# Reordering the six products of two channel tiles in a split-precision projection

## The chip, the cores and the metric

The kernel runs on one core of one Trainium2 chip. The metric is the device time of one execution in microseconds (us); times are compared by their medians over several runs.

## The reference

A decoder trunk of two residual layers over a sequence of 1024 tokens with 1024 channels, all in float32, and a final RMSNorm:

```
def reference(x, ...):
    for i in range(DEPTH):                       # DEPTH = 2
        h = rms_norm(x, norm_g[i])
        if i % N_MIXERS == 0:
            x = x + lru_mixer(h, ...)
        else:
            x = x + fox_mixer(h, ...)
    return rms_norm(x, final_g)

def lru_mixer(h, ...):                           # 1536 channels = 12 blocks of 128
    u = h @ w_in
    xb, gate = u[..., :1536], u[..., 1536:]
    xc = causal_depthwise_conv(xb, conv_w, conv_b)
    r = sigmoid(block_diag_linear(xc, wa, ba)); i = sigmoid(block_diag_linear(xc, wx, bx))
    a = exp(-8 * r * softplus(-a_param))
    hs = associative_scan(a, sqrt(1 - a**2) * (i * xc))
    return (hs * silu(gate)) @ w_out

def fox_mixer(h, ...):                           # 16 heads of 64
    q, k, v, gate, f_logit = split(h @ w_in)
    logits = q @ k.T / 8 + forgetting term from cumsum(log_sigmoid(f_logit)), causal
    return (softmax(logits) @ v * silu(gate)) @ w_out
```

## The kernel before

Activations are held with channels on the 128 partitions and tokens along the free dimension, in two halves of 512 tokens. A projection takes 8 channel tiles of 128 (12 for the output of the first layer, 8 for that of the second) into one accumulator of 128x512.

Each factor of such a product is split into a high part and a low part, and three of the four partial products are summed: high weights by high input, low weights by high input, high weights by low input. In layer 1 (the LRU layer) and in the output projections the parts are float32 values rounded for TensorE (`fp32r`, the rows show f32); in the query, key and gate projections of layer 2 they are float16. The weights are the first factor of `matmul(o, w, x)`: they are loaded into the array (an LDWEIGHTS, engine PEld in the profile), and the input's 512 columns are streamed past them.

`gemm_steps` writes these products, and yields after every second channel tile, so that callers can lay other work between. Its callers, by the name of what they accumulate:

- `product`: `ups` and `gps`, the branch and the gate path of the LRU layer, 12 channel blocks `n`, weights `wh`/`wl`, inputs `hh`/`hl`. `ups` is used by the convolution, `gps` by the SiLU.
- `gates`: `gate`, the two block-diagonal gates of a channel block, weights `wgh`/`wgl`, inputs `xch`/`xcl`. Here the list has one pair only, and the same matrices are used for both halves of the tokens.
- `project_out`: `ops`, the first layer's output, two channel blocks at a time, inputs `yh`/`yl` (the last two blocks are written by `mm3`, elsewhere).
- `play`: `gps1` (printed as `gps` with inputs `h` and weights `w`, f16), the query, key and gate projections that fill the attention of layer 2.
- `partial`: `ops1` (printed as `ops` with `yhh`/`yhl`), most of the second layer's output, near the end.

A weight block is loaded by SyncE's queue, cast to the high part by ScalarE (`to_hi`, L57), and the low part is the difference, made by GpSimd or VectorE (`to_lo`, L110). The low parts `hl`, `xcl`, `yl` of the inputs are made by VectorE after the high parts by ScalarE. Buffers rotate: 3 for the raw weights `wf`, 4 each for `wh` and `wl`.

The order on each engine in layer 1 is set by the framework's list scheduler from the program's order and its own timing model. In layer 2 the attention is interleaved by hand: strings such as `ORDER` say at which places a step of the scores (`maxima`: S, then p, pp and the transposing DMA into pT), of the weighted sum (`weigh`: O) or a step of the filling projections comes, and each step is held behind the last matmul written before it. The values projection (`values`: vps) has its own order of products.

Of the kernel before, what the change touches and what calls it, by code (L numbers as in the profile page):

```python
# [40 lines left out]
def trunk(ctx: ExitStack, tc: tile.TileContext, xt, w0, wg, wo0, pc, gn, gf, w1, wv, wf, bf, wo1, out):  # L41
# [26 lines left out]
    def matmul(*args, **kw):  # L68
        pe[0] = nc.tensor.matmul(*args, **kw)  # L69
        return pe[0]  # L70
# [66 lines left out]
    def gemm_steps(ps, pairs, chunks=(slice(0, HALF),)):  # L137

        pairs = list(pairs)
        for cs in chunks:  # L140
            o = ps[:, cs]
            for i, ((wh, wl), (xh, xl)) in enumerate(pairs):
                matmul(o, wh, xh[:, cs], start=i == 0, stop=False)
                matmul(o, wl, xh[:, cs], start=False, stop=False)
                matmul(o, wh, xl[:, cs], start=False, stop=i == len(pairs) - 1)
                if i % 2:
                    yield

    def drain(gen):
# [7 lines left out]
    def gemm(*args):  # L157
        drain(gemm_steps(*args))
# [40 lines left out]
    with nullcontext(ExitStack()) as l0:  # L199
# [184 lines left out]
        def out_weights(g, d0):  # L384

            wt = loaded([4, P])
            for j in range(2):
                nc.sync.dma_start(wt[:, 2 * j : 2 * j + 2], wo0[d0 + j, :, 2 * g : 2 * g + 2])
            hi = wpool.tile([P, 4, P], F32R, tag="wh", name="wh")
            lo = wpool.tile([P, 4, P], F32R, tag="wl", name="wl")  # L390
            to_hi(hi, wt, nc.scalar)
            to_lo(lo, wt, hi, nc.vector)
            return [[(hi[:, 2 * j + i], lo[:, 2 * j + i]) for i in range(2)] for j in range(2)]
# [184 lines left out]
        wl = [w for d0 in range(0, KT, 2) for w in out_weights(NB // 2 - 1, d0)]  # L578
        for h, cs in enumerate(halves):
# [4 lines left out]
            for d0 in range(0, KT, 4):  # L584
                pts = []
                for db in range(d0, d0 + 4):
                    if db % 2 == 0:
                        two = ps.tile([P, 2, HALF], F32, tag="S", name="ops")
# [31 lines left out]
    with ExitStack() as l1:  # L620
# [56 lines left out]
        def play(units):  # L677

            for u in units:
                u["start"]()  # L680
                w, h = u["w"], u["h"]
                after_ = [v["w"] for v in plan[plan.index(u) + 1 :] if v["w"] is not w][:1]
                pt = ps.tile([P, HALF], F32, tag="g", name="gps1")
                for i, _ in enumerate(gemm_steps(pt, zip(w.cast(), hT[h]))):
                    for v in after_ if seen[0] is not None else ():
                        if h == u["first"] and i == u["load"]:
                            v.load()
                        if h == u["last"] and i in u["cast"]:
                            with tc.issue_after(seen[0].ins):
                                v.cast(u["cast"].index(i) + 1)  # L690
                    yield
                nc.vector.scalar_tensor_tensor(pt, pt, unit_w[:, 4 + w.b : 5 + w.b], rs1[h], ALU.mult, ALU.mult)
                u["use"](h, pt)
# [406 lines left out]
        def partial(todo):  # L1100

            for db, c in todo:
                split_out(db)
                if c if db < 2 else not c:
                    split_out(db + 1)

                kept = c == 0 and db > 3
                x = home(db) if kept else rpool.tile([P, HALF], F32, tag="R", name="xp")
                nc.gpsimd.dma_start(x, x1d[c, :, db])
                pt = ps.tile([P, HALF], F32, tag="g", name="ops1")  # L1110
                yield from gemm_steps(pt, zip(wo[db], [y1[c][pair] for pair in range(6)]))
                nc.vector.tensor_tensor(x, x, pt, ALU.add)  # L1112
                if not kept:
                    nc.gpsimd.dma_start(x1d[c, :, db], x)
# [265 lines left out]
```

## Time and profile before

| | |
|---|---|
| median of 3 runs | 1066.17 us |
| the 3 runs | 1066.57, 1062.53, 1066.17 us |
| the profiled execution's own time | 1067.16 us |
| its span | 1065.4 us |
| TensorE matmuls | 1028.7 us busy (97%), 5094 records |
| TensorE weight loads | 721.8 us (68%), 5094 records |
| VectorE, ScalarE, GpSimd | 784.2, 659.9, 92.2 us |
| mean granted TensorE clock | 0.993 |

The span is the time from the first to the last instruction in the profile; 1.8 us of the execution's own time lie outside it. Matmuls are pipelined: the duration of one (0.39 us for 512 columns) is longer than the distance between two starts, so a stream is read by the distance of the starts. A fast matmul stream is one with no idle time in front of its members. The first layer ends at about 450 us, the attention runs from about 500 us, the last output quarter ends the span.

### The profile page before, as it was taken

How to read it: one execution, taken by the hardware profiler on the slowest of the kernel's cores; microseconds unless marked ns; L12 is line 12 of the kernel's file. 1: busy time of each engine (PE TensorE's matmuls, PEld its weight loads, DVE VectorE, ACT ScalarE, POOL GpSimd, SP SyncE). 2: the span in 40 equal slices, each digit the busy share in tenths (PEclk: the TensorE clock that was granted, in tenths of full speed). 3: DMA queues.
4: the chain of work that ended last, by engine and by line, in shares of the span. 5: the costliest groups of instructions: out<-in, count | busy, mean ns of one | idle time of the engine just before them, and what ended most of it. 6: DMA issues, size and time to landing. Idle time of an engine off the chain costs nothing. (4 is left out here: it accounts for less than half of the span.)

```text
span 1065.4 us, 15063 instructions
## 1 busy us (share of the span) xinstructions
PE 1028.7 (97%) x5094; PEld 721.8 (68%) x5094; DVE 784.2 (74%) x1456; ACT 659.9 (62%) x1211; POOL 92.2 (9%) x87
## 2 busy tenths in 40 slices
PE   9999999999999999998999989999999989999997
PEld 6787878888888888765445556554755448577776
DVE  7789667667856868885878866888487874986575
ACT  8479666565656575567657655675466664764455
POOL 1311111012103110001000000000000000012100
PEclk9999999999999999999999999999999999999999
DMA  7112434233423311543688993998658984789984
GB/s 244 60 49 63 117 88 128 78 114 112 134 65 121 112 58 40 170 130 87 150 163 171 180 198 80 192 179 176 163 106 180 180 190 120 151 194 240 250 199 159
DMA packets 219805, 148.92 MB, mean 140 GB/s; under 512 B 161936, under 2 KB 174864, under 8 KB 219728
## 3 DMA queue, kind: packets, MB, share of 16 engines
q1 hardware_dynamic: 217328, 140.09, 54.2%
q0 software_dynamic: 2400, 7.87, 2.4%
q8 instruction: 40, 0.66, 0.3%
q14 instruction: 37, 0.30, 0.1%
HBM read 73.33 MB, written 11.67 MB: 80 GB/s over the span
## 5 line engine op out<-in xcount | busy, mean ns | idle before, releaser
L69 PE MATMUL gps<-h,w 128*128 128x512 f16 x1152 | 269.1, 380 | 1.3 <-DVE qkl L795 1.1
L69 PEld LDWEIGHTS <-w 128*128 128x128 f16 x1152 | 104.2, 98 | 126.4 <-issue 13.8
L57 ACT ACTIVATE p<-S,m 128x128 f32<-128x128 f32 (+7 forms) x128 | 94.5, 739 | 68.1 <-DVE m L965 30.6
L57 ACT ACTIVATE pp<-p,sums 128x128 f16<-128x128 f32 (+7 forms) x128 | 96.0, 769 | 34.7 <-DVE sums L977 18.5
L979 DVE SCALAR_TENSOR_TENSOR pp<-p,sums,pp 128x128 f16<-128x128 f32 (+7 forms) x128 | 102.5, 813 | 14.1 <-ACT pp L57 11.7
L69 PE MATMUL S<-T,U 96*128 96x512 f32 (+7 forms) x384 | 106.2, 385 | 5.0 <-ACT p L57 4.7
L69 PE MATMUL vps<-w,h 128*128 128x256 f16 (+1 forms) x768 | 92.3, 282 | 12.7 <-ACT w L57 8.3
L965 DVE CUSTOM_DVE_ANT_0 S<-S,mask 128x128 f32<-128x128 f32 (+7 forms) x128 | 96.9, 758 | 6.1 <-PE S L69 5.3
L110 POOL TENSOR_TENSOR wl<-wf,wh 128x512 fp32r<-128x512 f32 x46 | 70.9, 1545 | 324.3 <-ACT wh L57 254.3
L69 PEld LDWEIGHTS <-h 128*128 128x128 f16 x768 | 76.7, 101 | 28.0 <-issue 10.8
L69 PEld LDWEIGHTS S<-T,U 128*128 128x128 f32 (+1 forms) x384 | 67.7, 190 | 28.8 <-ACT p L57 13.6
L57 ACT CAST wh<-wf 128x512 fp32r<-128x512 f32 x88 | 51.7, 593 | 53.6 <-PE ops L69 27.1
L69 PE MATMUL ops<-yh,wh 128*128 128x512 f32 x192 | 76.8, 400 | 0.9 <-ACT yh L57 0.5
L69 PE MATMUL ups<-hh,wl 128*128 128x512 f32 x192 | 75.8, 395 | 1.8 <-POOL wl L110 1.8
L69 PE MATMUL ups<-hh,wh 128*128 128x512 f32 x192 | 76.4, 399 | 0.7 <-ACT hh L57 0.6
L69 PE MATMUL O<-pT,v 128*128 128x512 f16 (+3 forms) x396 | 71.0, 322 | 6.0 <-DMA pT<-pp 6.0
L69 PE MATMUL gps<-hh,wh 128*128 128x512 f32 x192 | 75.7, 394 | 0.8 <-ACT wh L57 0.8
L69 PE MATMUL ups<-hl,wh 128*128 128x512 f32 x192 | 76.1, 396 | 0.1
L69 PE MATMUL ops<-yh,wl 128*128 128x512 f32 x192 | 75.7, 394 | 0.1
L69 PE MATMUL gps<-hh,wl 128*128 128x512 f32 x192 | 75.5, 393 | 0.0
L69 PE MATMUL gps<-hl,wh 128*128 128x512 f32 x192 | 75.5, 393 | 0.0
L69 PE MATMUL ops<-yl,wh 128*128 128x512 f32 x192 | 74.6, 394 | 0.0
(196 smaller groups left out, 1883.5 us busy)
## 6 DMA issues: line engine op xcount, KB each, us to landing
wf<-in_w SPq DMA_DIRECT2D x106, 256.0 KB
wsf<-in_w SPq DMA_DIRECT2D x48, 256.0 KB
wf<-in_wo SPq DMA_DIRECT2D x64, 128.0 KB
T<-qkh SPq DMA_DIRECT2D x64, 128.0 KB
U<-qkh SPq DMA_DIRECT2D x64, 128.0 KB
x<-in_xt SPq DMA_DIRECT2D x16, 256.0 KB
wsf<-in_wv SPq DMA_DIRECT2D x16, 256.0 KB
x1d<-x SPq DMA_DIRECT2D x16, 256.0 KB
```

Of the source, the lines that this page charges most:

```text
L57: act[0] = op(*args, **kw)
L69: pe[0] = nc.tensor.matmul(*args, **kw)
L110: return eng.tensor_tensor(lo, src, f32(hi), ALU.subtract)
L965: nc.vector.tensor_tensor_reduce(S[:, :n], S[:, :n], mask[:, SEQ - n :], -1.0, -NEG, ALU.add, ALU.min, accum_out=m)
L979: nc.vector.scalar_tensor_tensor(both[:, :, 1], p, r, both[:, :, 0], ALU.mult, ALU.subtract)
```

## The change

In `gemm_steps` the channel tiles are taken two at a time. Before, each tile's three products stood together, in the order high by high, low weights by high, high weights by low input. Now, of two tiles, first come the two products of each tile with the weights' high part (by the input's high part, then by its low part), four in all; then the two with the weights' low parts. With a single pair (in `gates`) the order becomes high by high, high by low input, low by high. The number of products, their operands, the accumulators and the places of the yields stay.

```
-            for i, ((wh, wl), (xh, xl)) in enumerate(pairs):
-                matmul(o, wh, xh[:, cs], start=i == 0, stop=False)
-                matmul(o, wl, xh[:, cs], start=False, stop=False)
-                matmul(o, wh, xl[:, cs], start=False, stop=i == len(pairs) - 1)
-                if i % 2:
+            for i in range(0, len(pairs), 2):
+                two = pairs[i : i + 2]
+                for j, ((wh, wl), (xh, xl)) in enumerate(two):
+                    matmul(o, wh, xh[:, cs], start=i + j == 0, stop=False)
+                    matmul(o, wh, xl[:, cs], start=False, stop=False)
+                for j, ((wh, wl), (xh, xl)) in enumerate(two):
+                    matmul(o, wl, xh[:, cs], start=False, stop=i + j == len(pairs) - 1)
+                if len(two) == 2:
                     yield
```

What stands on the engines follows from this and from the scheduler. Three places on TensorE are shown; the numbers behind the names tell the buffers apart (`hh_171`/`hl_172` are the two parts of channel tile 0, `hh_173`/`hl_174` of tile 1; `wh_130`/`wl_131` are the weights of `ups`, `wh_139`/`wl_140` those of `gps`).

First, the start of the program behind the warm-up, where `ups` and `gps` of channel block 0 are interleaved. Before:

```order
L69 MATMUL ups_239<-hh_171,wh_130 128x512
L69 MATMUL ups_239<-hh_171,wl_131 128x512
L69 MATMUL ups_239<-hl_172,wh_130 128x512
L69 MATMUL ups_239<-hh_173,wh_130 128x512
L69 MATMUL ups_239<-hh_173,wl_131 128x512
L69 MATMUL ups_239<-hl_174,wh_130 128x512
L69 MATMUL gps_264<-hh_171,wh_139 128x512
L69 MATMUL ups_239<-hh_175,wh_130 128x512
L69 MATMUL ups_239<-hh_175,wl_131 128x512
L69 MATMUL gps_264<-hh_171,wl_140 128x512
```

And with the change, at the same place:

```order
L69 MATMUL ups_239<-hh_171,wh_130 128x512
L69 MATMUL ups_239<-hl_172,wh_130 128x512
L69 MATMUL ups_239<-hh_173,wh_130 128x512
L69 MATMUL ups_239<-hl_174,wh_130 128x512
L69 MATMUL ups_239<-hh_171,wl_131 128x512
L69 MATMUL ups_239<-hh_173,wl_131 128x512
L69 MATMUL gps_264<-hh_171,wh_139 128x512
L69 MATMUL gps_264<-hl_172,wh_139 128x512
L69 MATMUL gps_264<-hh_173,wh_139 128x512
L69 MATMUL gps_264<-hl_174,wh_139 128x512
L69 MATMUL ups_239<-hh_175,wh_130 128x512
L69 MATMUL gps_264<-hh_171,wl_140 128x512
```

The low input part `hl_172` is now second, where it was third; the low weights come fifth and sixth. Of `gps`, four products stand ahead of the next tile `hh_175` of `ups`, where one did.

Second, TensorE at the start of `ups` of channel block 5 (weights `wh_1290`/`wl_1291`; `ops` are products of the first layer's output). Before:

```order
L69 MATMUL ups_1300<-hh_171,wh_1290 128x512
L69 MATMUL ups_1300<-hh_171,wl_1291 128x512
L69 MATMUL ups_1300<-hl_172,wh_1290 128x512
L69 MATMUL ups_1300<-hh_173,wh_1290 128x512
L69 MATMUL ups_1300<-hh_173,wl_1291 128x512
```

With the change:

```order
L69 MATMUL ups_1300<-hh_171,wh_1290 128x512
L69 MATMUL ups_1300<-hl_172,wh_1290 128x512
L69 MATMUL ups_1300<-hh_173,wh_1290 128x512
L69 MATMUL ups_1300<-hl_174,wh_1290 128x512
L69 MATMUL ops_1130<-yh_591,wh_1118 128x512
L69 MATMUL ops_1130<-yl_592,wh_1118 128x512
L69 MATMUL ops_1130<-yh_771,wh_1118 128x512
L69 MATMUL ops_1130<-yl_772,wh_1118 128x512
L69 MATMUL ops_1130<-yh_591,wl_1119 128x512
L69 MATMUL ops_1130<-yh_771,wl_1119 128x512
L69 MATMUL ups_1300<-hh_171,wl_1291 128x512
L69 MATMUL ups_1300<-hh_173,wl_1291 128x512
```

Before, the product with the low weights `wl_1291` was the second of the block. Now four products with `wh_1290` and six of `ops` stand ahead of it.

Third, a projection in layer 2 (float16: `h16` and `w16` each hold both parts of a tile, so that the parts are not told apart by name). Here the weight loads are instructions of their own. Before:

```order
L69 LDWEIGHTS w16_4244
L69 MATMUL gps1_4239<-h16_3640,w16_4244 128x512
L69 LDWEIGHTS w16_4244
L69 MATMUL gps1_4239<-h16_3640,w16_4244 128x512
L69 LDWEIGHTS w16_4244
L69 MATMUL gps1_4239<-h16_3640,w16_4244 128x512
L69 LDWEIGHTS w16_4244
L69 MATMUL gps1_4239<-h16_3641,w16_4244 128x512
L69 LDWEIGHTS w16_4244
L69 MATMUL gps1_4239<-h16_3641,w16_4244 128x512
```

With the change:

```order
L69 LDWEIGHTS w16_4244
L69 MATMUL gps1_4239<-h16_3640,w16_4244 128x512
L69 LDWEIGHTS w16_4244
L69 MATMUL gps1_4239<-h16_3640,w16_4244 128x512
L69 LDWEIGHTS w16_4244
L69 MATMUL gps1_4239<-h16_3641,w16_4244 128x512
L69 LDWEIGHTS w16_4244
L69 MATMUL gps1_4239<-h16_3641,w16_4244 128x512
L69 LDWEIGHTS w16_4244
L69 MATMUL gps1_4239<-h16_3640,w16_4244 128x512
L69 LDWEIGHTS w16_4244
L69 MATMUL gps1_4239<-h16_3641,w16_4244 128x512
```

The products are in the new order, and each still has its own load. Counted over the whole program, both versions have the same instructions on every engine. Outside TensorE, 71 of 1435 rows of VectorE, 55 of 968 of ScalarE, 24 of 724 of SyncE and 2 of 92 of GpSimd stand elsewhere. Nearly all of these are in layer 1, in heads 13 to 15 and behind them; in the attention between these no row of VectorE, ScalarE, SyncE or GpSimd moves, and TensorE's units (each accumulator's group of products) follow one another as before.

## The prediction

> **What bounds the kernel now.** I read the page's head first, then busy time by stages, then the rows of the stages.
>
> ```profile
> span 1065.4 us, 15063 instructions
> PE 1028.7 (97%) x5094; PEld 721.8 (68%) x5094; DVE 784.2 (74%) x1456; ACT 659.9 (62%) x1211; POOL 92.2 (9%) x87
> ```
>
> TensorE (PE) is busy for 97% of the span, no other engine for more than 74%. Weight loads (PEld) are as many as matmuls. By stages (columns: length, then busy us and count of PE, PEld, DVE, ACT, POOL, then the granted clock, the DMA share, GB/s):
>
> ```profile
> 0.00:50.00 50.00, 47.50 (x192) 36.66 (x193) 35.21 (x42) 33.57 (x53) 11.59 (x14) 1.00 0.48 160
> 50.00:100.00 50.00, 49.86 (x216) 40.09 (x214) 46.22 (x60) 37.88 (x46) 6.27 (x4) 1.00 0.17 47
> 100.00:200.00 100.00, 97.43 (x416) 77.64 (x417) 63.19 (x69) 64.80 (x131) 18.13 (x12) 1.00 0.35 104
> 200.00:300.00 100.00, 100.00 (x435) 81.28 (x434) 73.43 (x75) 60.27 (x100) 16.54 (x11) 1.00 0.35 111
> 300.00:400.00 100.00, 100.00 (x434) 81.38 (x433) 67.34 (x68) 64.33 (x100) 19.11 (x12) 1.00 0.29 92
> ...
> 800.00:900.00 100.00, 93.16 (x524) 55.63 (x523) 72.14 (x173) 59.02 (x114) 0.00 (x0) 0.97 0.82 177
> 900.00:1000.00 100.00, 100.00 (x483) 69.65 (x482) 77.44 (x179) 58.79 (x115) 12.52 (x23) 1.00 0.84 195
> ```
>
> From 200 to 400 us TensorE never stands idle: 434 matmuls in 100 us, 0.230 us from start to start. There only a cheaper matmul would help, and only a new wait would hurt. TensorE is idle for 2.50 us up to 50 us, 0.14 us up to 100 us and 2.57 us up to 200 us; from 800 to 900 us it is idle for 6.84 us.
>
> **The matmuls themselves: 0 us.** The change gives each TensorE instruction the same operands, and moves 688 weight matrices so that the same one is loaded twice running: one for each pair of channel tile and token half. The counts come from these groups of the page's and the grouped rows (192 + 192 + 192 + 96 + 48 = 720, less the 32 of `ops` that `mm3` writes: 8 output tiles x 2 halves x 2 blocks).
>
> ```profile
> L69 PE MATMUL ups<-hl,wh 128*128 128x512 f32 x192 | 76.1, 396 | 0.1
> ...
> L69 PE MATMUL gps<-hl,wh 128*128 128x512 f32 x192 | 75.5, 393 | 0.0
> ...
> L69 PE MATMUL ops<-yl,wh 128*128 128x512 f32 x192 | 74.6, 394 | 0.0
> ...
> L69 PE MATMUL ops<-yhl,wh 128*128 128x512 f32 x96 | 37.9, 395 | 0.0
> ...
> L69 PE MATMUL gate<-xcl,wgh 128*128 128x512 f32 x48 | 18.0, 395 | 0.0
> ...
> L69 PEld LDWEIGHTS ups<-hl,wh 128*128 128x128 f32 x192 | 36.1, 188 | 9.4 <-DVE hl L265 1.1 <-issue 0.2
> ```
>
> What a repeated matrix is worth is in the trace already. A gate's last product in one token half and its first in the next use the same `wgh` (the loop over halves keeps `w`). The time order at 300 us (start, duration):
>
> ```profile
> 299.98 0.39 PE L69 MATMUL gate<-xcl,wgh 128*128 128x512 f32 x1
> 300.21 0.40 PE L69 MATMUL gate<-xch,wgh 128*128 128x512 f32 x1
> 300.45 0.39 PE L69 MATMUL gate<-xch,wgl 128*128 128x512 f32 x1
> 300.68 0.40 PE L69 MATMUL gate<-xcl,wgh 128*128 128x512 f32 x1
> ...
> 300.21 0.19 PEld L69 LDWEIGHTS gate<-xch,wgl 128*128 128x128 f32 x1
> ...
> 648.21 1.47 PE L69 MATMUL gps<-h,w 128*128 128x512 f16 x6
> ```
>
> From 299.98 to 300.21 the matrix stays, and the step is 0.23 us; from 300.21 to 300.45 it changes, and the step is 0.24. The load of 0.19 us runs beside the matmul that starts with it (both at 300.21). So a repeat gains nothing, and costs nothing. In float16 six matmuls take 1.47 us: five steps of (1.47 - 0.39) / 5 = 0.216 us (0.39 us for the last, as the f32 rows have), against 0.230 in f32. Were a repeat's f32 step as short as an f16 step, it would gain 0.014 us; this is the upper bound, 688 x 0.0144 = 9.9 us, and a rival below. A loss per repeat is excluded by the same step of 0.23. I take 0, the row itself. [...] Here the order with the change still has a load ahead of every matmul, and the trace hides the load anyway.
>
> **Waits that the change shortens.** TensorE's waits in layer 1 behind a weight's or an input's part:
>
> ```profile
> 8.94 0.49 PE L69 MATMUL gps<-hh,wh 128*128 128x512 f32 x1 [0.75 <-ACT wh L57]
> 9.66 0.51 PE L69 MATMUL ups<-hh,wh 128*128 128x512 f32 x1 [0.23 <-ACT hh L57]
> ...
> 104.63 0.49 PE L69 MATMUL ups<-hh,wl 128*128 128x512 f32 x1 [0.42 <-POOL wl L110]
> ...
> 143.54 0.39 PE L69 MATMUL ups<-hh,wh 128*128 128x512 f32 x1
> 145.31 0.50 PE L69 MATMUL ups<-hh,wl 128*128 128x512 f32 x1 [1.38 <-POOL wl L110]
> ```
>
> - At 145.31 the second product of the block waits 1.38 us for GpSimd's low weights. Now nine more products stand ahead of it (three of the block, six of `ops`). The scheduler moved the whole block earlier too, so that not all nine are cover; I count the three that the change itself puts there: 3 x 0.23 = 0.69 us. Bounds 0 and 1.38.
> - At 104.63 the same wait of 0.42 us; three products cover it: 0.42 us.
> - From 8.94 to 9.66 TensorE does one `gps` product and waits for the next input tile. Now it has four there, and 0.72 - 0.23 = 0.49 us of the step is used. The 0.75 us ahead of it stays: it is the cast of the `gps` weights, which is as late as before.
>
> Together 1.6 us.
>
> **Waits that it lengthens.** The low input part comes second of six instead of third, and of the second tile fourth instead of sixth. In most of layer 1 it is `hl`, made once, long ago. It is fresh only at the start:
>
> ```profile
> 10.71 0.68 DVE L283 TENSOR_TENSOR m<-m,ti 128x512 f32<-128x512 f32 x1
> ...
> 11.92 0.74 DVE L265 SCALAR_TENSOR_TENSOR hl<-x,gnt,hh 128x512 fp32r<-128x512 f32 x1
> ```
>
> Per channel tile VectorE spends 0.74 + 0.68 = 1.42 us there, and TensorE six products (`ups` and `gps`) of 0.23 = 1.39 us: neither gets ahead. With both accumulators interleaved, the low part of the second tile moves from the 11th of twelve places to the 7th or so: up to 4 x 0.23 = 0.92 us of wait, once, since TensorE stays behind afterwards. Against it stands the slack that it had; bounds 0 and 0.92, and I take 0.7. Behind TensorE's wait is only TensorE's own queue. For `yl` and `xcl` in the blocks up to 180 us I take 0 in the forecast, and their price in the rival. Beyond 200 us TensorE has no idle time, so that the other engines are ahead.
>
> **Layer 2 and the end: 0 us.** The idle time there ends by ScalarE's softmax, the transposing DMA or the casts of the values' weights, and these rows are among the largest:
>
> ```profile
> 625.73 4.53 PE L69 MATMUL vps<-w,h 128*128 128x256 f16 x40 [2.66 <-ACT w L57]
> ...
> 750.45 5.76 PE L69 MATMUL vps<-w,h 128*128 128x256 f16 x36 [2.18 <-ACT w L57]
> ...
> 878.28 7.94 PE L69 MATMUL vps<-w,h 128*128 128x256 f16 x45 [3.48 <-ACT w L57]
> ...
> 1002.39 1.04 PE L69 MATMUL O<-pT,v 128*128 128x512 f16 x4 [1.54 <-DMA pT<-pp]
> ```
>
> None of them waits for a product's inner order, and `values` has an order of its own. On SyncE some weight loads pass the transposes of the last head, but the last of these keeps its place; bounds -1 and +1 us (the wait of 1.54 at 1002.39 is the nearest), value 0.
>
> **The clock.** The waits at 750.45 and 878.28 were followed by a halved clock, that of 2.66 us at 625.73 was not (same columns as in the stages):
>
> ```profile
> 751.00:754.50 3.50, 3.50 (x19) 2.44 (x17) 1.62 (x3) 1.05 (x2) 0.00 (x0) 0.51 0.90 188
> 877.50:884.00 6.50, 5.72 (x28) 3.93 (x28) 2.83 (x4) 3.51 (x5) 0.00 (x0) 0.50 0.97 215
> ...
> 600.00:700.00 100.00, 95.90 (x562) 58.14 (x561) 74.57 (x182) 61.82 (x121) 0.00 (x0) 1.00 0.75 160
> ```
>
> That is 3.5 x 0.49 + 6.5 x 0.50 = 5.0 us of lost clock. A longer wait did not bring it where a shorter one did, so that it can come or go with a small shift in time: -5.0 to +3.2 us (one more like the second). [...]
>
> **The sum.** On the profiled execution's own time, 1067.16 us (the span of 1065.4 and 1.8 around it): 1067.16 - 0.69 - 0.42 - 0.49 + 0.7 = 1066.3. This execution lies 1.0 us above the median of the three runs, 1066.17, so that the forecast for a median is **1065.3 us**: no change that a measurement of this kernel can tell, which takes about 0.5%, or 5.3 us.
>
> **The rivals.**
>
> - *A repeated matrix is cheaper* (faster): 9.9 us off, 1055.4. For it speaks only that f32 steps are longer than f16 steps; the gate rows, where the matrix repeats, speak against it. Chance 0.06.
> - *The clock stays up* (faster): without either half-clock stretch 1065.3 - 5.0 = 1060.3. The shift of layer 1 would have to miss both; nothing at those waits changes. Chance 0.08.
> - *VectorE's low parts come late in the early blocks* (slower). Up to 180 us TensorE has little lead: all its waits quoted from layer 1, and the 2.57 us lost from 100 to 200 us, lie there. Now `yl` and `xcl` are wanted a product or two earlier, and the scheduler has moved 71 rows of VectorE, mostly here. One of its operations is
>
> ```profile
> 102.20 1.22 DVE L110 TENSOR_TENSOR xcl<-xc,xch 128x1024 fp32r<-128x1024 f32 x1
> ```
>
>   If TensorE waits one such operation longer in each of the blocks 0 to 5, this is 6 x 1.22 = 7.3 us, 1072.6 us. It decides from the point at which VectorE ends a low part after TensorE has done the products ahead of it, and the wait recurs in at least four blocks (4.9 us and the rest of the sum). Against it: GpSimd's waits show the weights late there, not the inputs. Chance 0.20.
>
> That the change does not do what it says can be left out: the order shows the new sequence in every unit.
>
> **How the numbers follow.** The forecast has the rest, 0.66. Faster by over 0.5%: 0.06 + 0.08 = 0.14; slower: 0.20; within: 0.66. The range goes from the case of the clock, 1060.0, to the whole price of the slower rival, 1072.6; it leaves out the cheaper matrix (0.06) and what is worse than the slower rival's price.
>
> **What would show it.** In the profile after: f32 steps of 0.23 us and f16 steps of 0.216 wherever `hh,wh` and `hl,wh` follow each other; as many PEld records as PE; 434 matmuls from 300 to 400 us again; the waits at 104.63 and 145.31 shorter or gone; the waits of `vps` and of O as long as before. Wrong would be: f32 steps near 0.216 (cheaper matrix), a full clock from 700 to 900 us (the clock), or waits of `ops`, `gate` or `ups` for DVE's yl, xcl or hl of 5 us in sum before 200 us.

## The result, and the profile after

| | before | after |
|---|---|---|
| median, 9 runs each | 1065.75 us | 1073.72 us |
| lowest to highest | 1060.75 to 1068.01 | 1068.84 to 1076.51 |
| profiled execution's own time | 1067.16 us | 1073.72 us |
| its span | 1065.4 us | 1072.0 us |
| mean granted TensorE clock | 0.993 | 0.989 |

The ratio after to before is 1.0084, with a 95% interval of 1.0066 to 1.0102: the change makes the kernel about 9 us slower (the two medians differ by 8.0 us). The measured 1073.72 us lies above the predicted range (1060.0 to 1072.6), and no change had been forecast.

The head of the profile after, and its busy time by stages (columns as before: length, busy us and count of PE, PEld, DVE, ACT, POOL, the granted clock, DMA share, GB/s):

```profile
span 1072.0 us, 15085 instructions
PE 1031.0 (96%) x5094; PEld 724.5 (68%) x5094; DVE 788.3 (74%) x1456; ACT 660.9 (62%) x1211; POOL 94.7 (9%) x87
0.00:50.00 50.00, 47.74 (x190) 37.13 (x191) 36.38 (x42) 33.57 (x53) 11.76 (x14) 0.97 0.46 158
50.00:100.00 50.00, 50.00 (x218) 40.73 (x217) 46.04 (x58) 35.46 (x44) 9.83 (x5) 1.00 0.16 49
300.00:400.00 100.00, 100.00 (x434) 81.04 (x433) 66.94 (x68) 64.30 (x100) 18.98 (x12) 1.00 0.28 92
900.00:1000.00 100.00, 100.00 (x480) 69.50 (x478) 76.84 (x178) 58.67 (x114) 12.54 (x23) 1.00 0.86 190
```

The matmuls cost what they did: 434 from 300 to 400 us, as before. In the first 50 us the granted clock, 1.00 before, is 0.97. What is new beyond that are waits. TensorE's largest new ones in layer 1 and the one that decides the end, in order of time:

```profile
139.69 0.50 PE L69 MATMUL ups<-hh,wh 128*128 128x512 f32 x1 [1.31 <-ACT wh L57]
148.41 0.50 PE L69 MATMUL ops<-yh,wh 128*128 128x512 f32 x1 [0.78 <-DVE x L406]
436.77 0.50 PE L69 MATMUL ops<-yh,wl 128*128 128x512 f32 x1 [0.71 <-DVE wl L110]
1006.96 1.87 PE L69 MATMUL O<-pT,v 128*128 128x512 f16 x4 [6.79 <-DMA pT<-pp]
```

The last row answers to the one at 1002.39 before, where the same four matmuls waited 1.54 us and took 1.04. The wait is 5.25 us longer, and the matmuls behind it run at half the clock:

```profile
1007.00:1012.00 5.00, 5.00 (x13) 3.38 (x14) 2.13 (x5) 2.44 (x5) 0.00 (x0) 0.52 0.72 220
```

These 5 us lose 5 x 0.48 = 2.4 us. Before, the clock is full there:

```profile
1000.00:1020.00 20.00, 18.46 (x87) 13.49 (x86) 11.33 (x25) 8.25 (x16) 3.24 (x6) 1.00 0.89 242
```

The wait and the clock make 7.6 us, more than the 6.6 us between the two spans. What else is lost does not show in this pair of traces, because the execution traced before reaches 508 us late (the latest of five traces with the old layer 1, below); it takes the further runs to see it.

**Who is late at the end.** O waits for the transposing DMA of head 14's last two blocks (`pp_9315`, `pp_9359`). SyncE's queue, before and then after (start, duration of the issue; two transposes in a row):

```profile
991.71 8.68 SPq L982 DMA_TRANSPOSE pT<-pp  x2
```

```profile
990.57 14.31 SPq L985 DMA_TRANSPOSE pT<-pp  x2
```

They start 1.1 us earlier than before and end 4.5 us later. Most of it is in the second of the two, 9.4 us instead of 4.4 (the first takes 4.9 instead of 4.1). SyncE waits for no semaphore there; what differs is what else the DMA engines carry: GpSimd's queue (q0 in the DMA view) takes 28.2 and 22.2% of their time in the two windows of 5 us from 990 us before, and 30.0, 68.0 and 31.3% in the three after. GpSimd's instructions before:

```profile
984.72 1.06 POOL L1109 DMA_DIRECT2D x<-x1d  x2 [1.20 <-PE S L69]
989.46 0.54 POOL L1109 DMA_DIRECT2D xp<-x1d  x1 [3.68 <-DMA x1d<-xp]
989.99 0.54 POOL L1109 DMA_DIRECT2D x<-x1d  x1
```

and after:

```profile
989.70 0.54 POOL L1112 DMA_DIRECT2D xp<-x1d  x1 [5.90 <-DMA x1d<-xp]
990.39 1.59 POOL L1112 DMA_DIRECT2D x<-x1d  x3
```

These loads fetch the accumulators of the last output tiles in `partial`: `xp` for a tile that is stored again (it has to wait until an earlier store has freed its buffer), `x` (buffer `x4`) for a tile that stays. The program order of GpSimd's queue has changed by one place. Before:

```
L1114 DMA x1d_94<-xp_9266 128x512
L1109 DMA x4_9445<-x1d_94 128x512 x2
L1109 DMA xp_9510<-x1d_94 128x512
L1109 DMA x4_9445<-x1d_94 128x512
```

After:

```
L1117 DMA x1d_94<-xp_9266 128x512
L1112 DMA xp_9510<-x1d_94 128x512
L1112 DMA x4_9445<-x1d_94 128x512 x3
```

`xp_9510` waits for the store of `xp_9266`, and behind it now wait all three loads of `x4`, 256 KB each. Before, two of them were under way at 984.72, ahead of the transposes; after, all three start at 990.39, together with them. The DMA views of the two windows, 995 to 1000 us before and 1000 to 1005 us after, while TensorE waits or is about to:

```profile
DMA packets 2141, 1.30 MB, mean 260 GB/s; under 512 B 1843, under 2 KB 1843, under 8 KB 2140
```

```profile
DMA packets 1474, 0.64 MB, mean 128 GB/s; under 512 B 1402, under 2 KB 1402, under 8 KB 1474
```

All queues together move half as much in the same time. No run here shows a transpose's own rate: of the 1.30 MB behind the 260 GB/s, 0.43 MB are GpSimd's.

The bytes alone do not make the delay. The two loads that are new beside the transposes hold 0.52 MB, 2.0 us at 260 GB/s, and the two transposes take 5.6 us longer; why the rate fell as well stays open.

So three theories stood at this point. **Theory 1:** GpSimd's load queue makes the end late. **Theory 2:** SyncE's queue does it, where the change puts a weight load ahead of the transpose of `pp_9286` and four ahead of that of `pp_9412`. **Theory 3:** the order of the products costs it elsewhere. A fourth came out of the first four runs: layer 1 itself costs 2 to 3 us.

### The profile page after: what moved, and what is told of

It is laid out like the page before. It is cut to its first block, busy times and chain, and to the rows that moved or that the text cites. A ratio compares the mean times of both kernels' runs of the same rounds, so it can differ in the third digit from the quotient of the medians.

```text
span 1072.0 us, 15085 instructions
## 1 busy us (share of the span) xinstructions
PE 1031.0 (96%) x5094; PEld 724.5 (68%) x5094; DVE 788.3 (74%) x1456; ACT 660.9 (62%) x1211; POOL 94.7 (9%) x87
## 5 line engine op out<-in xcount | busy, mean ns | idle before, releaser
L69 PEld LDWEIGHTS <-w 128*128 128x128 f16 x1152 | 104.2, 98 | 126.8 <-issue 14.1
L110 POOL TENSOR_TENSOR wl<-wf,wh 128x512 fp32r<-128x512 f32 x46 | 73.4, 1599 | 322.3 <-ACT wh L57 285.7
L69 PEld LDWEIGHTS S<-T,U 128*128 128x128 f32 (+1 forms) x384 | 67.7, 190 | 28.2 <-ACT p L57 13.1
L406 DVE TENSOR_TENSOR x<-x,ops 128x512 f32<-128x512 f32 x80 | 53.8, 679 | 29.8 <-PE ops L69 29.5
L650 DVE SCALAR_TENSOR_TENSOR w<-wf,wsq,w 128x512 f16<-128x512 f32 (+1 forms) x74 | 54.6, 750 | 25.0 <-ACT w L57 24.9
L69 PEld LDWEIGHTS <-v 128*128 128x128 f16 x396 | 36.6, 98 | 50.4 <-issue 15.0
```

Source lines behind the costliest of these rows:

```text
L110: return eng.tensor_tensor(lo, src, f32(hi), ALU.subtract)
L650: nc.vector.scalar_tensor_tensor(lo, wt, scales[:, b : b + 1], hi, ALU.mult, ALU.subtract)
```

## The experiments

The measured values stand together in this table. "Layer 1" says where the changed order of the products is used in layer 1; the ratio is to the kernel before, run on the same chip. "First S" is the start of the first S product in the trace, the end of layer 1 and of the preparations of layer 2. "Pair" is SyncE's time for the two transposes, "wait" that of O behind them.

| run | layer 1 | layer 2 | median, us | ratio, 95% interval | first S | pair | wait |
|---|---|---|---|---|---|---|---|
| before | old | old | 1065.75 | | 508.34 | 8.68 | 1.54 |
| after | new | new | 1073.72 | 1.0084 (1.0066 to 1.0102) | 508.76 | 14.31 | 6.79 |
| e1 | new | new, old load queue | 1072.62 | 1.0046 (1.0027 to 1.0065) | 510.92 | 8.54 | (below) |
| e2 | old | old, new load queue | 1071.88 | 1.0046 (1.0027 to 1.0065) | 507.20 | 14.64 | 5.17 |
| e3 | old | new in `partial` | 1072.62 | 1.0057 (1.0038 to 1.0075) | 507.25 | 14.09 | 5.87 |
| e4 | new | new but `partial` | 1070.64 | 1.0028 (1.0010 to 1.0046) | 509.47 | 8.59 | 1.71 |
| e5 | new | old | 1070.81 | 1.0040 (1.0023 to 1.0057) | 509.46 | 8.57 | 1.78 |
| e6 | old | new in `play` | 1067.41 | 1.0016 (0.9995 to 1.0036) | 506.70 | 8.68 | 1.82 |
| e7 | old | old, loads in order | 1066.16 | 1.0000 (0.9982 to 1.0018) | 506.46 | 8.71 | 0.69 |
| e8 | new | new, loads in order | 1069.54 | 1.0039 (1.0021 to 1.0056) | 510.26 | 9.03 | 1.53 |
| e9 | `ups`, `gps` | old | 1069.72 | 1.0039 (1.0021 to 1.0058) | 509.06 | 8.78 | 1.92 |
| e11 | `ops` | old | 1067.46 | 1.0016 (0.9998 to 1.0034) | 508.49 | 8.70 | 1.55 |
| e12 | `gate` | old | 1068.31 | 1.0020 (0.9998 to 1.0041) | 508.19 | 8.59 | 1.82 |
| e13 | new but first block, `gate` | new, loads in order | 1066.98 | 1.0018 (1.0003 to 1.0032) | 507.57 | 8.82 | 0.69 |

### The load queue against SyncE's queue: e1 to e4

The first two exchange GpSimd's queue between the kernels. e1 takes the changed kernel and loads `x4` in the old order:

```
...
+                if db == 5 and c == 0:
+                    for d in (5, 6):
+                        home_load[0] = nc.gpsimd.dma_start(home(d), x1d[0, :, d])
+                elif (db, c) in ((5, 1), (7, 0)):
+                    with tc.issue_after(home_load[0].ins):
+                        home_load[0] = nc.gpsimd.dma_start(x, x1d[c, :, db])
+                elif (db, c) != (6, 0):
+                    nc.gpsimd.dma_start(x, x1d[c, :, db])
...
```

> The changed order of the products throughout; only GpSimd's DMA queue is put back near 985 us to the order of the kernel before: two home loads x4, then the load xp_9510 that waits for a store, then the third x4. SyncE's queue keeps the changed order there (a weight load ahead of the transpose of pp_9286, four weight loads ahead of that of pp_9412). Theory 1, the home loads, held behind xp_9510, run into the transposes of the last head pair: the wait of O <- pT,v at about 1000 us falls from 6.79 us to between 1.0 and 2.5, its four matmuls from 1.87 us to about 1.04, and the time is 1064 to 1067 us, at most that of before. Theory 2, SyncE's order (a weight load ahead of a transpose) makes the transposes late: the wait stays at 6 to 7 us, the time at 1072 to 1075. Theory 3, the order of the products itself costs it on TensorE or VectorE: 1072 to 1075 too.

e2 takes the kernel before and puts the waiting load first:

```
+                if (db, c) == (5, 0):
+                    ahead = rpool.tile([P, HALF], F32, tag="R", name="xp")
+                    home_load[0] = nc.gpsimd.dma_start(ahead, x1d[1, :, 5])
...
+                    with tc.issue_after(home_load[0].ins) if kept and db > 4 else nullcontext():
+                        nc.gpsimd.dma_start(x, x1d[c, :, db])
```

> The kernel before with the old order of the products; only GpSimd's DMA queue has the changed order near 985 us: the load that waits for the store of xp_9266 stands ahead of the three home loads x4. SyncE's queue stays as before at the transposes of pp_9248 to pp_9359. Theory 1 (the queue of GpSimd): the wait of O <- pT,v at about 1000 us grows from 1.54 us to 5 to 7.5, and the time to 1071 to 1075 us. Theory 2 (SyncE's order) and theory 3 (the products themselves): the wait stays at 1.0 to 2.5 us and the time at 1064 to 1067.

e3 and e4 split the change itself: `gemm_steps` gets a flag for the order, set in `partial` alone or everywhere else.

```
+    def gemm_steps(ps, pairs, chunks=(slice(0, HALF),), tiles_two=False):
...
-                yield from gemm_steps(pt, zip(wo[db], [y1[c][pair] for pair in range(6)]))
+                yield from gemm_steps(pt, zip(wo[db], [y1[c][pair] for pair in range(6)]), tiles_two=True)
```

> The changed order only in the partial output products of layer 2's second part (the generator partial); everywhere else the old one. Both queues then stand at the end as in the changed kernel. Theories 1 and 2: the wait of O <- pT,v at about 1000 us is 5 to 7.5 us, and the time 1071 to 1075 us, about 0.7 above the changed kernel at most, since the waits that layer 1 lost are back. Theory 3 in the form that the products of layer 1 and of the other layer-2 products cost it: 1064 to 1067.

> The changed order everywhere but in partial, which keeps the old one; both queues then stand at the end as in the kernel before. Theories 1 and 2: the wait of O <- pT,v is 1.0 to 2.5 us, and the time 1064 to 1066.5 us: 0 to 1 below before, by the waits that layer 1 loses (the span is 0.7 ahead at 997 us in the changed kernel). Theory 3 (layer 1 or the other products cost it): 1070 to 1075.

SyncE's pair of transposes and O's wait in e2, then the pair in e1:

```profile
987.34 14.64 SPq L982 DMA_TRANSPOSE pT<-pp  x2
1004.00 1.89 PE L69 MATMUL O<-pT,v 128*128 128x512 f16 x4 [5.17 <-DMA pT<-pp]
```

```profile
999.04 8.54 SPq L985 DMA_TRANSPOSE pT<-pp  x2
```

In these runs the pair takes 8.54 to 8.68 us wherever the two `x4` loads stand ahead of `xp_9510`, and 14.09 to 14.64 where they stand behind it, with either order of the products and of SyncE's queue. e2, which changes nothing else, is 0.46% slower: theory 1 holds for the transposes, and its price is 4.9 us (0.0046 x 1066.7; 2.9 to 6.9 by the interval). Theory 2 falls: in e1 SyncE has the changed order near the end, and the pair takes 8.54 us.

But the times of e1 and e4 missed. Both should have come back to the time of before, and they were 0.46% and 0.28% slower. In e1 the end is late in another way, a wait of S, because ScalarE's cast of a weight waits for its load and holds the softmax queued behind it (TensorE's row, then ScalarE's):

```profile
1001.52 0.95 PE L69 MATMUL S<-T,U 128*128 128x384 f32 x2 [2.43 <-ACT p L57]
```

```profile
999.23 0.62 ACT L57 CAST wh<-wf 128x512 fp32r<-128x512 f32 x1 [2.67 <-DMA wf<-in_wo]
```

In e4 the end is as before, so that another part of the change costs something ahead of it: theory 3 is true as well. The traces of old and new layer 1 already part by the first S (table), and that gave theory 4, the cost of layer 1 itself, its place.

### Layer 1 and the f16 products apart: e5, e6

The same flag, now set in layer 1 alone, and in `play` alone.

> The changed order in layer 1 alone (up, gate and output products); layer 2's products, and both queues at the end, as before. Theory 4, from the profiles of the four runs before this one: layer 1 itself costs 2 to 3 us, by a clock of about 0.83 from 5 to 15 us, the waits near 140 and 148 us for wh and x, 0.4 ns per matmul, and the wait for wl at 437: so 1068 to 1070.5 us, and O's wait at about 1002 stays at 1.5 to 2 us. Rival, the prediction's sum for layer 1 (shorter waits, 0.9 us gained): 1064.5 to 1067.

> The changed order only in the f16 products of layer 2 that fill TensorE beside attention (the generator play); layer 1, partial and both queues at the end as before. Theory 4: the time of before within 1.5 us, 1065 to 1068. Rival, the f16 products are what e4 still loses: 1069 to 1071.

Layer 1 alone costs 0.40%, 4.3 us, with an interval that leaves out zero and so the gain of the sum; the median, 1070.81, is even 0.3 us above what theory 4 expected. `play` alone is inside what can be resolved (its interval just holds 1). In e5 TensorE's waits near 140 and 148 us are those of the changed kernel:

```profile
140.03 0.50 PE L69 MATMUL ups<-hh,wh 128*128 128x512 f32 x1 [1.70 <-ACT wh L57]
148.98 0.51 PE L69 MATMUL ops<-yh,wh 128*128 128x512 f32 x1 [1.01 <-DVE x L423]
```

The five traces with the whole new layer 1 (after, e1, e4, e5, e8) reach the first S at 509.77 us on average, the five with the old one (before, e2, e3, e6, e7) at 507.19: 2.6 us. TensorE's waits, added up from each trace up to there, are 8.97 us against 7.16, so 1.8 us of it. By place, new against old: 0 to 20 us 1.31 against 0.97; 90 to 135 us 0.46 against 1.16 (the gain that the prediction saw); 135 to 160 us 2.47 against 1.14; from 435 us on 4.67 against 3.85. The rest is in slower matmuls: the clock at the start (below), in e1 alone a second stretch of half clock from 141.5 to 144.9 us, and steps of 230.7 ns against 230.3 (some 1170 of them from 150 to 421 us, 0.4 us).

Where the 2.6 us arise shows when TensorE's products are counted and the start of the same count is compared, again five traces against five. The new layer 1 is 1.0 us late by 18 us. It gains 1.6 us between 98 and 123 us, loses 1.9 us between 137 and 155 us, 0.6 us more up to 425 us, 0.6 us at 437 us, and 0.2 us up to 468 us. The rest, from 2.6 to the 4.3 us of the median, lies behind the first S and is spread over waits of layer 2 that also differ between traces with the same layer 1; it was not traced to a place.

### How much the bytes beside the transposes matter: e7, e8

Each load of the last tiles is queued behind the one before, in the order of their products. That puts the last `x4` load behind the transposes, but the second one beside them:

```
...
-                nc.gpsimd.dma_start(x, x1d[c, :, db])
+                with tc.issue_after(loads[-1].ins) if db > 4 else nullcontext():
+                    loads.append(nc.gpsimd.dma_start(x, x1d[c, :, db]))
```

> The old order of the products; GpSimd's loads of the last four output tiles each queued behind the one before, in the order in which their products are made: x4, xp_9510, x4, xp_9593, x4. One 256 KB load less runs beside the transposes of pp_9315 and pp_9359. Theory 1, the loads share the DMA engines with the transposes: those two take 5 to 8 us in place of 8.68, O's wait at about 1002 is 0 to 1 us in place of 1.54, and the time is 0 to 2 us below before. Rival, the transposes are late only where a waiting load has been queued ahead, whatever the bytes: 8.7 us and the time of before.

> The changed order of the products throughout, with GpSimd's loads queued as in the run before this one; SyncE's queue about as in the changed kernel. Theory 1: the two transposes take 5 to 8.7 us in place of 14.31, O's wait is 0 to 2.5 us, and the end costs at most 1 us over the kernel before; with theory 4's 2 to 3 us for layer 1 the time is 1067 to 1070.5. Rival, SyncE's order costs the end: 1072 to 1075.

With the old products the time does not move (1.0000). O's wait falls to 0.69 us, as theory 1 said, but the pair stays at 8.71 us, not 5 to 8: it was also the rival's number. One `xp` and one `x` load still start beside the transposes, at 988.61 and 989.14, and that is what the kernel before has at 989.46 and 989.99. So the edit did not take a load away from the transposes, and the two explanations were not told apart: what fewer than two loads would do was not run. With the new products the queue takes back what the end had lost:

```profile
991.47 9.03 SPq L985 DMA_TRANSPOSE pT<-pp  x2
```

```profile
1002.59 1.02 PE L69 MATMUL O<-pT,v 128*128 128x512 f16 x4 [1.53 <-DMA pT<-pp]
```

The changed kernel goes from 1.0084 to 1.0039, and what stays is the price of layer 1 in e5, 1.0040. SyncE still has five weight loads ahead of the transpose behind the pair in this kernel (one before, four in the changed kernel), which settles theory 2.

### Layer 1 by kinds of product: e9 to e12

The flag in `ups` and `gps` alone, in `gate` alone, in `ops` alone.

> The changed order only in layer 1's products of inputs and weights (ups, gps); the gate's three products, the output products, layer 2 and both queues as before. In the five traces with the old layer 1 the first S product starts at 506.5 to 508.3 us (mean 507.2), in the five with the new one at 508.8 to 510.9 (mean 509.8). Theory 4a, the loss of 2.6 us is in this part: clock 0.83 from 5 to 15 us, waits for hl near 7 us, first S 508.3 or later. Theory 4b, it comes with the gate's products, whose new order lets other units go first: clock 1.00 in that stretch, first S at 507.2 within 0.7.

> The changed order only in the gate's three products (tile xch, xcl by wgh, then wgl), four gates to a block; every other product old. On TensorE the gate blocks then move against the rest (that of 140 us goes behind an up product, as in the changed kernel). Theory 4b: the waits from 135 to 160 us are 2 to 2.8 us in place of 0.8 to 1.7, and the first S starts at 508.3 or later. Theory 4a: those waits are 0.8 to 1.7 us, the first S at 507.2 within 0.7, and the time that of before.

> The changed order only in layer 1's output products (ops); every other product old. If the waits from 435 us to the first S (3.8 to 4.05 us with the old order, 4.5 to 4.95 with the new) come from these products, they are 4.5 or more here, with one of 0.71 us for wl at 437, and the first S starts at 507.7 to 508.5. If they come from the moved units, there is no such wait, and the first S starts at 507.2 within 0.7. The time is that of before in both cases, within 1.5 us.

The traced execution of e10 took 1727.22 us at a mean clock of 0.556, so its trace is not read; its other runs gave 1.0023 (1.0003 to 1.0043). The same kernel went again as e12.

> The kernel of the run before last again (the changed order only in the gate's three products), for a profile at full clock. Theory 4b, the gates' new order moves units and that costs the waits at 140 and 148 us: from 135 to 160 us TensorE waits 2 to 2.8 us (old 0.8 to 1.7), clock 1.00 from 5 to 15 us, first S at 507.5 to 509. Rival, only the new inner order of all three kinds together brings these waits: 0.8 to 1.7 us, first S at 507.2 within 0.7.

`ups` and `gps` alone cost 0.39%, about all of layer 1, and theory 4a holds: the first S starts at 509.06, 1.9 us of the 2.6 behind the mean of the old layer 1. The stage from 5 to 15 us in before, e9, e11 and e12:

```profile
5.00:15.00 10.00, 8.66 (x32) 5.65 (x30) 7.81 (x11) 8.96 (x17) 2.73 (x2) 1.00 0.96 329
```

```profile
5.00:15.00 10.00, 8.31 (x27) 5.83 (x27) 7.73 (x10) 8.47 (x17) 3.11 (x2) 0.83 1.00 352
```

```profile
5.00:15.00 10.00, 8.11 (x28) 4.95 (x28) 7.77 (x10) 8.57 (x17) 3.10 (x2) 1.00 1.00 351
```

```profile
5.00:15.00 10.00, 8.67 (x32) 5.36 (x30) 7.72 (x10) 8.51 (x17) 3.10 (x2) 1.00 0.99 352
```

Only e9 has the low clock of 0.83. All six traces in which the first block has the new order have it there, and all eight others that can be read have 1.00.

Theory 4b falls as it was written: with the new order in `gate` alone TensorE waits 1.12 us from 135 to 160 us, as with the old order, and e9 1.29. The waits at 140 and 148 us need the parts together. e12's first S, 508.19, is where theory 4b put it (507.5 to 509) and above the rival's 507.9, so that each of the two was right in one point. Its units have moved, and it waits elsewhere, in sum 1.86 us from 90 to 135 us against 1.16:

```profile
100.93 0.50 PE L69 MATMUL ups<-hh,wl 128*128 128x512 f32 x1 [0.86 <-POOL wl L110]
120.02 0.50 PE L69 MATMUL gps<-hh,wh 128*128 128x512 f32 x1 [0.99 <-ACT wh L57]
```

The wait for `wl` at 437 us is in e11 (0.71 us), as expected, but also in e9, where `ops` has the old order:

```profile
437.10 0.50 PE L69 MATMUL ops<-yh,wl 128*128 128x512 f32 x1 [0.72 <-DVE wl L110]
```

So the new inner order of `ops`, which wants `wl` fifth instead of second, is not needed for it; the low weights themselves come later there in both kernels. Which instruction of VectorE moved ahead of them was not tried. e11's waits from 435 us on are 4.42 us, just under the 4.5 expected if they came from `ops`, its first S is at 508.49, and its time 1.9 us above before, 0.4 us more than expected and not resolved (the interval holds 1).

### All three places at once: e13

New order everywhere but in the first block's products and in `gate`, with the loads in program order:

```
...
-            gemm(pt, zip(w, raw[h]))
+            gemm(pt, zip(w, raw[h]), tiles_two=bool(state))
...
+                    gemm(pt, [(w, tuple(z[:, cs] for z in s["x"]))], tiles_two=False)
...
```

> The changed order everywhere but in the products of layer 1's first block and in the gates, and GpSimd's loads of the last output tiles queued in program order. If the three places account for the whole loss (the start with its halved clock, the units moved by the gates, the load queue at the end): clock 1.00 from 5 to 15 us, waits of 0.8 to 1.7 us from 135 to 160, transposes under 9.1 us, and the time of before within 2 us, 1064.5 to 1068. If something spread over all the products costs too, 1068.5 to 1071.

The clock from 5 to 15 us is 1.00, TensorE waits 0.33 us from 135 to 160 us, the pair takes 8.82 us and O waits 0.69 us. The loss goes from 0.84% to 0.18% (0.03 to 0.32). The three places together account for most of it (e8 gives the queue's share; the first block and `gate` were not tried one without the other); some 2 us stay, with an interval that just leaves out zero, and no place was found for them. No kernel of the study was faster than the one before.

## Why the prediction was wrong

- **"Layer 2 and the end: 0 us", with bounds of -1 and +1: the step that failed, by its size.** The text looked at SyncE's queue, found that the last transpose keeps its place, and stopped there. The moved rows of GpSimd's queue were only counted. That queue decides which loads run beside the transposes: by itself it costs 0.46% in e2, 4.9 us, and the wait it lengthens grew by 5.25 us in the changed kernel's trace. The bound was taken from the wait's own length of 1.54 us, but in e2, where only GpSimd's load queue was changed, the wait is 5.17 us, and in the changed kernel 6.79.
- **"Waits that the change shortens: 1.6 us": right at the places named, wrong as a sum.** The waits at 104.63 and 145.31 for GpSimd's low weights are gone. New ones stand close by (139.69, 1.31 us; 148.41, 0.78 us): the block that started at 143.54 without a wait now starts at 139.69 and waits for its high weights. The prediction had noted that the block moves ahead, and counted it only on the gain's side. Over five traces each, the waits from 135 to 160 us went from 1.14 to 2.47 us: +1.3 where -0.7 was predicted. With the start, a layer 1 that was to gain 0.9 us (the whole sum) lost 2.6.
- **The start: 0.7 - 0.49 = 0.2 us predicted, 1.0 us by 18 us measured.** TensorE waits for `hl` twice for 0.29 us, which is near the 0.7 by luck: it was worked out for a low part that moves from the 11th place to the 7th, and the order shows that of the second tile going from sixth to fourth. The waits at 8.94 and 9.66 us, from which the credit of 0.49 was taken, are gone in the changed kernel, but over five traces each the waits to 20 us rose by 0.34 us, and the halved clock behind them (0.50 from 8.32 to 11.74 us in the changed kernel) makes most of the rest; the prediction considered the clock only in layer 2.
- **The matmuls: 0 us, nearly right.** 434 in 100 us. A closer count has 0.4 ns more for each, 0.4 us from 150 to 421 us. The cheaper repeated matrix did not appear.
- **The slower rival did not happen.** Its mechanism, low parts of the inputs from VectorE late in the blocks up to 180 us, would have shown 5 us of waits for `yl`, `xcl` or `hl`; there are 0.58 us, all for `hl`. It gave nearly the measured time, 1072.6 us, and was wrong all the same.
- **The clock** was named as a term that can come or go. In layer 2 it did both: a half clock came at 626 us for 3.4 us and one at 881 us went, so that the 0 taken for it came out there. It also came at two places that were not in the term, at the start and behind O's long wait (2.4 us). (The lower end of the range, 1060.0, is the clock rival's 1060.3 taken a little lower.)

The single parts add to more than the whole: 0.40 (layer 1), 0.16 (`play`) and 0.57 (`partial`) make 1.13% against 0.84% measured. Perhaps a delay in one hides part of another; that was not tried, `play`'s 0.16 is not resolved, and the interval of `partial` holds the 0.46 of the queue alone. Layer 1 alone (e5, 0.40) and the load queue alone (e2, 0.46) add to 0.86%, what the whole change costs.

## What to carry to other kernels

An edit inside a helper is also an edit to every queue that a scheduler fills around it: compare the order of all queues that carry DMAs, and for each load that waits ask what is queued behind it and what that will meet when it starts late. The length of a wait today did not bound it here: O's wait for the transposing DMA was 1.54 us before, 5.17 with the other load queue alone, 6.79 with the whole change. And where traces with the same layer 1 differ by 2 us at its end (506.46 to 508.34), a place has to be read from several of them; one pair showed only the end here and hid layer 1.

## What the runs showed of the hardware

- Two transposes of 128x14x128 and 128x16x128 took 8.5 to 9.0 us on SyncE's queue beside two loads of 256 KB from GpSimd's, and 14.1 to 14.6 us beside four (`xp` and three `x4`); a store of 256 KB from GpSimd's queue ran beside them in each of these traces. All queues together moved 306, 260 and 249 GB/s in the three windows of 5 us from 990 us before, and 334, 151 and 128 GB/s with four loads.
- TensorE's clock fell to half without a long wait. In the changed kernel the longest wait from 5 to 8.5 us is 0.61 us, and yet the three windows from 8 us on are:

```profile
8.00:8.50 0.50, 0.43 (x2) 0.34 (x3) 0.50 (x2) 0.49 (x1) 0.00 (x0) 0.82 0.92 311
8.50:11.50 3.00, 3.00 (x9) 2.32 (x8) 2.32 (x4) 2.96 (x6) 1.29 (x1) 0.50 1.03 383
11.50:12.00 0.50, 0.50 (x3) 0.46 (x2) 0.50 (x2) 0.50 (x2) 0.00 (x0) 0.76 1.06 389
```

  With the shares of the first and the last window the half clock lasts 3.0 + 0.18 + 0.24 = 3.4 us, from 8.32 us on. e11 had a longer wait there, 0.86 us, and kept the full clock:

```profile
7.70 0.50 PE L69 MATMUL ups<-hh,wh 128*128 128x512 f32 x1 [0.86 <-ACT hh L57]
```

  The trace's record of the clock has this stretch as 3.413 us. TensorE was not idle for such a length ahead of it: from 4.91 to 8.32 us, the 3.41 us before the half clock, it was busy for 2.22 us.

- In these traces a half clock goes with how busy TensorE was in one stretch of 3.41 us ahead of it, not with how long it waited. Each trace's record of the clock changes in steps of 3.41 us (in the kernel before, from 6.95 to 1061.67 us, it is full for 218 of them, half for 1, full for 36, half for 2, full for 52), and so lays a row of windows through the trace. Behind the start, in the fourteen traces that can be read, each of the windows at full clock with less than 1.37 us of TensorE's busy time was followed by half clock, and none with more than 1.49 us. The kernel before has a wait of 2.66 us at 625.73 that is split between two windows (1.73 and 2.45 us busy) and kept the full clock; in the changed kernel the same wait, 2.62 us at 626.45, lies almost wholly in one (1.10 us busy), and half clock followed.

  In the window at the start the bound lies higher, which was not explained: half clock followed 1.88 to 2.26 us of busy time in the six traces with the new first block, and did not follow 2.36 to 2.87 us in seven of the other eight. The eighth is e11, with 2.19 us from 3.94 to 7.35 us; that window still holds products of the warm-up, and the wait of 0.86 us lies across its end.
